# Query columns rotated once for all heads, sorts by 32, row passes on VectorE and a new order at the start of attention

## The chip, the cores and the metric

One core of a Trainium2 chip runs the whole program. The metric is the device time of one execution in microseconds. The kernel before takes 3343.34 us (median of three runs, 3342.88 to 3346.71).

## The reference

A trunk of two layers on 1024 tokens of width 1024, all in float32:

```python
for l in range(DEPTH):                                   # DEPTH = 2
    mod = silu(c) @ w_mod[l] + b_mod[l]                  # sh1, sc1, g1, sh2, sc2, g2
    h = rmsnorm(x, norm1_g[l]) * (1 + sc1) + sh1
    cq, ckv, kr, pu, cx, cb, cc, gl = split(h @ w_in[l])  # 5792 columns
    # attention: q = rmsnorm(cq) @ w_uq, 8 heads of 64 plain + 32 rotated columns;
    # k = [64 plain columns per head, 32 rotated columns shared], v 64 per head; softmax over 1024 keys
    ya = attention(cq, ckv, kr) @ w_oa[l]
    yb = pooling(pu) ; yc = short_convolution(cx, cb, cc) @ w_oc[l]
    merged = gate0 * ya + gate1 * yb + gate2 * yc        # gates = sigmoid(gl + b_gate)
    x = x + g1 * (merged @ w_out[l])
    h2 = rmsnorm(x, norm2_g[l]) * (1 + sc2) + sh2
    aff = softmax(h2 @ w_router[l])                      # 16 experts
    top_val, top_idx = top_k(aff.T, 128)                 # each expert takes its 128 best tokens
    x = x + g2 * scatter_add(swiglu(h2[top_idx]) * top_val)
return rmsnorm(x, final_g)
```

A rotation takes the two halves x1, x2 of the 32 columns to x1 cos - x2 sin and x1 sin + x2 cos.

## The kernel before, in words

Every large product is done as three matmuls (`mm3`, line 325): both factors are split (`split`, line 115) into a part `hi` that ScalarE rounds to the matmul's format and the rest `lo` that VectorE subtracts, and hi·hi + hi·lo + lo·hi are summed in PSUM. So each weight block and each activation costs one pass of ScalarE and one of VectorE.

The order of the instructions on each engine is laid out when the program is built, from the order in which they are written and from when the planner believes their inputs ready; each engine then works through its own list. `behind(ins)` puts what is written in it behind an instruction on the same engine, `gated(ins, by)` makes one wait for another. DMAs are issued from the queue of the engine named: SP for most loads, POOL for stores, ACT for some.

A layer runs through these stages:

1. Projections from `h` (held transposed, `hhi`, `hlo`), the convolution and the pooling.
2. Low-rank projections `cq`, `ckv` and the key's 32 rotated columns (lines 695 to 722), then the eight projections of the attention's gate (line 755 and after). Beside these, `w_out` is multiplied by g1 (`wk`, line 766) and gates go to DRAM (line 770).
3. Attention. A unit is one head and one tile of 128 queries: `scores`, softmax, `trans` (eight transposes, split again), and after each second unit `av`. Scores run two units ahead (LA = 2). `k_pair(hp)` makes the plain key rows of two heads and splits the pair's query weights into `qw`, in seven pieces for hi and lo. `q_head(h)` makes 128 rows of one head's query: 64 plain, 32 rotated columns, and the same 32 with their halves swapped. The rows are multiplied by a table (`tab_e` or `tab_o`: ones, cosine, signed sine) and split. The keys hold the rotated 32 rows twice (`rope_part`, one for each of four key buffers), so the product over 128 rows sums both parts of the rotation.
4. The merges: sixteen products with `w_oa` (`merge_mm`), each gated and added to the other branches (`merge_gate`). The gates come from DRAM two ahead (`gate_load`).
5. The output projection, eight tiles of 128 tokens (`out_mm`), each with a residual sum (`xo`), a norm, transposes (`x_trans`), `router`, `soft` (the 16 affinities of each token) and `h2_rows`: the normed rows go to DRAM for the experts, ScalarE scaling them, POOL multiplying by `a2` and adding `sh2`.
6. Routing. The 128 best affinities of each expert are found by sorting. `LISTS` are lists of one or two tiles, sorted by 16 rounds of "eight largest" and "replace" on 16 partitions (`top_round`). Tiles 6 and 7 take the quick way: `quick_sort` spreads the 128 tokens over four groups of 32 on 128 partitions, `quick_rounds` sorts these in four rounds, `quick_gather` brings them back to 16 partitions, `quick_list` merges them in steps of a bitonic sort, `quick_merged` merges the list into the best so far. Work of the lists is put in `fill` and taken out FILL steps at a time, twice a tile. After the last tile the threshold, the slots (`choose`, `chosen`) and the first gather follow.
7. The experts: 16 rounds of three products with 1024x1024 weights, loaded through a ring of buffers.

## Time and profile before

| | |
|---|---|
| median of three runs | 3343.34 us |
| the profiled execution | 3343.92 us |
| its span, first to last instruction | 3342.1 us |
| TensorE busy (matmul) | 3178.8 us, 15825 instructions |
| VectorE busy | 2434.5 us, 3738 instructions |
| ScalarE busy | 1857.3 us, 2535 instructions |
| POOL busy | 346.5 us, 356 instructions |
| mean granted clock of TensorE | 0.979 of full speed |

The first number is measured without the profiler; the profiled execution has its own time, and the span lies within it. Busy time is what the engine spent in instructions, without waits. In the views below, "L115" is a line of the kernel. A name such as `wlo<-raw,whi` is output and inputs. PE is TensorE's matmul, PEld its weight load, DVE is VectorE, ACT is ScalarE, SP the queue that issues most loads. "Idle before" and "waited for" name what ended an engine's idle time.

### The profile page before, as it was taken

To read this page: it belongs to the slowest core of one execution; us is meant where nothing else is said; L and a number is where in the kernel's file an instruction comes from. 1 tells how busy PE (TensorE), PEld (TensorE's weight loads), DVE (VectorE), ACT (ScalarE), POOL (GpSimd) and SP (SyncE) were. 2 spreads that over 40 slices of the span, in tenths; PEclk is the share of its full clock that TensorE was granted. 3 is DMA by queue.
4 is the path that set the end of the run, shared out by engine and by line. 5 is a ranking of instruction groups with operands and counts; after the bars stand their busy time and mean duration, and the time that the engine had idled before them with its cause. 6 is when DMAs were issued, how large, how long until landed. Compare 5 with 4: busy or idle time off the path is not lost.

```text
span 3342.1 us, 41527 instructions
## 1 busy us (share of the span) xinstructions
PE 3178.8 (95%) x15825; PEld 2616.3 (78%) x15825; DVE 2434.5 (73%) x3738; ACT 1857.3 (56%) x2535; POOL 346.5 (10%) x356
## 2 busy tenths in 40 slices
PE   6999999999997999999989999999999969999996
PEld 5888887788786788888778888887887858888875
DVE  5555525499868899999854445347998589999997
ACT  5111213488744888887631122226886448888876
POOL 2001011000023001010020000010000331001010
PEclk8999999999998999999999999999999979999998
DMA  6346334100366899999622354340005659999995
GB/s 225 120 138 205 130 125 137 64 18 7 117 221 233 314 394 380 389 389 373 245 60 82 128 165 139 104 164 24 14 28 164 227 211 366 390 390 380 387 381 182
DMA packets 279271, 685.90 MB, mean 205 GB/s; under 512 B 24934, under 2 KB 131648, under 8 KB 279072
## 3 DMA queue, kind: packets, MB, share of 16 engines
q1 hardware_dynamic: 242912, 563.13, 45.5%
q0 software_dynamic: 33856, 111.74, 10.6%
q10 hardware_dynamic: 2304, 8.39, 0.7%
q8 instruction: 124, 2.03, 0.2%
q14 instruction: 75, 0.61, 0.1%
HBM read 607.63 MB, written 75.55 MB: 204 GB/s over the span
## 4 chain that ended last, share of the span: by engine, by line
PE 79%; DVE 12%; ACT 4%; issue 2%; DMA 2%; POOL 1%; SPq 0%; POOLq 0%; DVEq 0%; ACTq 0%
PE ps L325 63%; PE pa L325 4%; PE pa L1149 4%; DVE wlo L115 4%; DVE mx L846 2%; PE pa L864 2%; PE ps L1353 1%; PE pa L872 1%; PE pa L874 1%; ACT whi L115 1%; ACT pexp L851 1%; PE pa L1189 1%; DVE af L1072 1%; DVE pexp L854 1%; DVE T L115 0%
## 5 line engine op out<-in xcount | busy, mean ns | idle before, releaser
L115 DVE TENSOR_TENSOR wlo<-rg,whi 128x1024 fp32r<-128x1024 f32 x768 | 899.6, 1220 | 97.9 <-ACT whi L115 95.1
L115 ACT CAST whi<-rg 128x1024 fp32r<-128x1024 f32 x768 | 763.8, 1048 | 180.1 <-PE ps L325 180.0
L325 PE MATMUL ps<-whi,T 128*128 128x512 f32 x3072 | 841.5, 393 | 3.6 <-ACT T L115 2.2
L325 PEld LDWEIGHTS ps<-whi,T 128*128 128x128 f32 x3072 | 574.4, 189 | 125.6 <-ACT T L115 3.1
L325 PE MATMUL ps<-wlo,T 128*128 128x512 f32 x1536 | 488.1, 399 | 5.0 <-DVE wlo L115 2.6
L325 PE MATMUL ps<-hhi,whi 128*128 128x512 f32 x1376 | 427.3, 392 | 0.0
L325 PE MATMUL ps<-hlo,whi 128*128 128x512 f32 x1376 | 424.0, 389 | 0.0
L325 PE MATMUL ps<-hhi,wlo 128*128 128x512 f32 x1376 | 423.7, 389 | 0.0
L115 ACT CAST whi<-raw 128x2048 fp32r<-128x2048 f32 (+2 forms) x63 | 108.7, 1726 | 428.0 <-PE ps L325 370.5
L325 PEld LDWEIGHTS ps<-wlo,T 128*128 128x128 f32 x1536 | 281.0, 189 | 74.3 <-DVE wlo L115 18.6
L325 PEld LDWEIGHTS ps<-hhi,whi 128*128 128x128 f32 x1376 | 256.9, 188 | 58.8 <-issue 4.2
L325 PEld LDWEIGHTS ps<-hlo,whi 128*128 128x128 f32 x1376 | 258.3, 188 | 54.2
L325 PEld LDWEIGHTS ps<-hhi,wlo 128*128 128x128 f32 x1376 | 258.3, 188 | 54.1
L115 DVE TENSOR_TENSOR wlo<-raw,whi 128x2048 fp32r<-128x2048 f32 (+2 forms) x63 | 130.1, 2065 | 99.9 <-ACT whi L115 99.8
L325 PE MATMUL ps<-khi,raw 128*128 128x512 f32 x512 | 165.8, 405 | 7.2 <-ACT pexp L851 5.7
L115 DVE TENSOR_TENSOR wlo<-pa,whi 128x512 fp32r<-128x512 f32 x256 | 169.5, 681 | 1.1 <-ACT whi L115 0.9
L851 ACT ACTIVATE pexp<-ps,nm 128x1024 f32<-128x1024 f32 x128 | 143.2, 1119 | 30.3 <-DVE nm L848 27.8
L846 DVE TENSOR_REDUCE mx<-ps 128x1 f32<-128x1024 f32 x128 | 155.0, 1213 | 4.3 <-PE ps L325 3.5
L1446 POOL DMA_INDIRECT xres<-y,idx x30 | 72.5, 2416 | 779.4 <-DVE y L1445 779.4
L115 ACT CAST whi<-pa 128x512 fp32r<-128x512 f32 x256 | 139.6, 588 | 6.2 <-PE pa L864 5.0
L229 DVE SCALAR_TENSOR_TENSOR macc<-raw,csil,macc 128x256 f32<-128x256 f32 x280 | 135.0, 484 | 8.4
L864 PE MATMUL pa<-ident,pexp 128*128 128x128 f32 x1024 | 135.2, 273 | 2.6 <-DVE nm L848 1.8
(412 smaller groups left out, 4626.9 us busy)
## 6 DMA issues: line engine op xcount, KB each, us to landing
rg<-in_w_gate_dram SPq DMA_DIRECT2D x128, 1024.0 KB, 8.9
rg<-in_w_up_dram SPq DMA_DIRECT2D x128, 1024.0 KB, 7.0
rg<-in_w_down_dram SPq DMA_DIRECT2D x128, 1024.0 KB, 7.8
raw<-in_w_mod_dram SPq DMA_DIRECT2D x48, 1024.0 KB, 5.3
raw<-in_w_in_dram SPq DMA_DIRECT2D x43, 1024.0 KB, 5.2
part<-pr POOLq DMA_DIRECT2D x32, 512.0 KB, 3.9
pr<-part POOLq DMA_DIRECT2D x16, 512.0 KB, 4.4
sq<-in_w_out_dram POOLq DMA_DIRECT2D x16, 512.0 KB, 4.7
```

The lines of the kernel that those rows point to most:

```text
L115: return ACT.copy(hi, src), DVE.tensor_sub(lo, src, f(hi))
L229: DVE.scalar_tensor_tensor(acc, raw[:, k], csil[:, k:k + 1], acc, op0=OP.mult, op1=OP.add)
L325: PE.matmul(dst[:, s], a, b[:, s], start=start and i == 0, stop=stop and i == 2)
L846: DVE.reduce_max(mx, p, axis=AX.X)
L851: ACT.activation(e, p, AF.Exp, bias=nm, scale=SCALE, accum_out=sm)
L854: DVE.tensor_scalar(e[:, :NORM_DVE], e[:, :NORM_DVE], ri, None, op0=OP.mult)
L864: PE.transpose(p[:, 128 * k:128 * k + 128], e[:, o:o + 128], ident)
L872: PE.matmul(po[:, o:o + 256], vt[:, k, h, :], phi[:, k, :], start=(k == 0), stop=False, skip_group_check=True)
L874: PE.matmul(po[0:64, o:o + 256], vt[:, k, h, 0:64], plo[:, k, :], start=False, stop=(k == 7), skip_group_check=True)
L1072: DVE.match_replace(a, v[:, 15 - r, :], a, -1.0)
L1149: PE.matmul(p[c_], a, b, start=(k == 0 and i == 0), stop=(k == 7 and i == 2))
L1446: POOL.indirect_dma_start(out=xres[l], in_=y, in_offset=None, compute_op=OP.add, out_offset=bass.IndirectOffsetOnAxis(ap=idx[e][:, 0:1], a ...
```

## The change

- Tables: `tabd` now has plain cosine, sine, and one table for the key (cosine and signed sine, twice). `krsel` writes the key's rotated rows once and zeros in the second copy.
- `q_rope`, written behind the gate projection of d = 3: from the 32 rotated columns of all heads it makes two blocks of 128 rows (first halves of all eight heads, second halves of all eight), rotates them, splits them, and stores hi and lo head by head in DRAM (`qrd`), by POOL's queue.
- `q_pair(hp)` in place of two `q_head`: the plain columns of two heads in one block of 128; the rotated rows of each head come from `qrd` by two loads of 32 partitions on SP, gated on an exponential some units back. A third query buffer `q3` is added; `q_head`'s product with a table goes, and `qw` is split in one piece.
- Start of attention: `k_pair(0)` and `q_pair(0)` are written ahead of the first value tiles; three of the four `rope_part` go into the unit loop at units 2, 9 and 17, behind an exponential; the first query weights are loaded during the gate projections.
- Merges: four products use PSUM that attention held, instead of two, and the split of `wo2` goes behind the split of the last head's output.
- Output projection: loads of the first two tiles on SP; transposes and router products written later; the rows of tiles 3 to 6 are scaled by VectorE in two instructions, those of tile 7 in a product after each half of the residual and one more instruction, ahead of the router's second half.
- Sorting: tiles 4 and 5 also take the quick way, two lists of two tiles remain, FILL goes from 4 to 6, and half of tile 6's sort is written ahead of the last softmax.
- `choose(0)` is made in two halves.

```diff
-FILL = 4
-LISTS = ((0, 2), (2, 2), (4, 1), (5, 1))
+FILL = 6
+LISTS = ((0, 2), (2, 2))
+OWN = 3
...
+            def q_rope(raw):
+                w = [W.tile([128, 3, 2, 8, 16], F32R, name=n_, tag=n_) for n_ in ("whi", "wlo")]
+                for i in range(2):
+                    split(w[0][:, :, i], w[1][:, :, i], raw[:, :, :, 16 * i:16 * i + 16])
+                w = [a.rearrange("p k i h c -> p k i (h c)") for a in w]
+                ps = []
+                for i in range(2):
+                    p = ps2()
+                    for k in range(3):
+                        mm3(p, w[0][:, k, i], w[1][:, k, i], cqhi[:, k], cqlo[:, k], k == 0, k == 2)
+                    ps.append(p)
+                cos, sin = (cp.tile([128, S], F32, name="sq", tag=n_, bufs=1) for n_ in ("sq", "rb"))
+                SP.dma_start(cos, tabd[0])
+                SP.dma_start(sin, tabd[1])
+                r = [cp.tile([128, S], F32, name="cf", tag="cf", bufs=3) for _ in range(3)]
+                hi = cp.tile([128, S], F32R, name="rhi", bufs=1)
+                for i, (a, b) in enumerate(((cos, sin), (sin, cos))):
+                    DVE.tensor_mul(r[2 * i], ps[0], a)
+                    DVE.tensor_mul(r[1], ps[1], b)
+                    (DVE.tensor_add if i else DVE.tensor_sub)(r[2 * i], r[2 * i], r[1])
+                    lo = r[2 * i].bitcast(F32R)
+                    split(hi, lo, r[2 * i])
+                    for part, src in enumerate((f(hi), r[2 * i])):
+                        POOL.dma_start(qrd[l][:, 16 * i:16 * i + 16, part, :], src)
...
+            def q_pair(hp):
+                w = [a.rearrange("p k i c -> p k (i c)") for a in qw[hp]]
+                for h in (2 * hp, 2 * hp + 1):
...
+                    r = 64 * (1 - h % 2)
+                    for o in (0, 32):
+                        ld = SP.dma_start(f(qs[h][r + o:r + o + 32]), qrd[l][h])
+                        if last_exp:
+                            gated(ld, last_exp[-4])
                 for q in range(2):
                     s_ = slice(512 * q, 512 * q + 512)
                     p = ps1()
                     for k in range(3):
-                        mm3(p, w[0][:, k, cc], w[1][:, k, cc], cqhi[:, k, s_], cqlo[:, k, s_], k == 0, k == 2)
-                    qf = ap.tile([128, 512], F32, name="pexp", tag="pexp", bufs=3)
-                    DVE.tensor_mul(qf, p, tab[:, s_])
-                    split(qs[h][:, 0, s_], qs[h][:, 1, s_], qf)
+                        mm3(p, w[0][:, k], w[1][:, k], cqhi[:, k, s_], cqlo[:, k, s_], k == 0, k == 2)
+                    for i in range(2):
+                        r = slice(64 * i, 64 * i + 64)
+                        split(qs[2 * hp + i][r, 0, s_], qs[2 * hp + i][r, 1, s_], p[r])
...
+            k_pair(0)
+            q_pair(0)
             for t in range(2):
                 v_tile(t)
-            k_pair(0)
-            q_head(0)
...
-            for i in range(1, 4):
-                rope_part(i)
             for n, (h, t) in enumerate(units):
+                if n in (2, 9, 17):
+                    with behind(last_exp[-1]):
+                        rope_part((2, 9, 17).index(n) + 1)
...
             for d in range(2):
-                merge_mm(pm[:, 512 * d:512 * d + 512], wo0, 128 * d, 0)
+                merge_mm(pms[d], wo0, 128 * d, 0)
             av(7, 3, *phl.pop((7, 3)), po[7])
+            for d in range(2, 4):
+                merge_mm(pms[d], wo1, 128 * d - 256, 0)
...
-        split(wo2[0], wo2[1], wo2_raw)
+        with behind(*last_o[-1]):
+            split(wo2[0], wo2[1], wo2_raw)
...
+                if t == 7:
+                    xn = gained.pop(t)
+                    DVE.scalar_tensor_tensor(xn, xn, rss[t], sh2, op0=OP.mult, op1=OP.add)
+                    return POOL.dma_start(h2d[l][sl, :], xn)
+                xn = op_.tile([128, D], F32, name="xn", bufs=1)
+                if t >= OWN:
+                    DVE.scalar_tensor_tensor(xn, xo, rss[t], a2, op0=OP.mult, op1=OP.mult)
+                    DVE.tensor_add(xn, xn, sh2)
+                else:
+                    with behind(softs[-1]):
+                        ACT.activation(xn, xo, AF.Copy, scale=rss[t])
+                    POOL.tensor_mul(xn, xn, a2)
+                    POOL.tensor_add(xn, xn, sh2)
...
             def aff_trans(t):
-                if t == 6:
+                if t > 3:
                     quick_sort(t)
                     quick_rounds(t)
...
             scale(t)
+            stored = h2_rows(t)
             router(t, 1)
-            quick_gather(6)
             fills(1000)
+            quick_half(6)
             ready = soft(t)
             quick_sort(t)
             quick_rounds(t)
             quick_gather(t)
+            with behind(ready):
+                quick_merged(6)
...
-            stored = h2_rows(t)
-            with behind(ready):
-                quick_merged(6)
```

## Rows read from the trace of the kernel before

**Rows 1.** The page, busy time by engine: us, share of the span, instructions.
```profile
PE 3178.8 (95%) x15825; PEld 2616.3 (78%) x15825; DVE 2434.5 (73%) x3738; ACT 1857.3 (56%) x2535; POOL 346.5 (10%) x356
```
**Rows 2.** Layer 0 by stretch: us; busy PE, PEld, DVE, ACT, POOL; PEclk, DMA, GB/s.
```profile
512.00:600.00 88.00, 88.00 (x382) 70.22 (x381) 49.37 (x34) 25.41 (x22) 12.86 (x24) 1.00 0.48 162
655.00:887.00 232.00, 229.29 (x1460) 200.04 (x1458) 216.00 (x431) 196.82 (x362) 1.60 (x3) 1.00 0.08 25
...
955.00:1062.00 107.00, 102.81 (x545) 85.10 (x545) 72.13 (x300) 51.30 (x96) 41.32 (x28) 1.00 0.56 214
1062.00:1097.00 35.00, 8.61 (x86) 7.26 (x87) 28.62 (x118) 14.13 (x27) 9.09 (x9) 0.53 0.61 217
```
**Rows 3.** TensorE's waits, whole span: waited for, us, times, longest us.
```profile
PE pa L325 <- DVE op L884: 9.8, 2, 4.9
...
PE ps L325 <- ACT pexp L851: 6.2, 8, 1.8
PE pa L1175 <- DVE xo L1154: 6.0, 4, 1.9
...
PE pa L1221 <- DVE aff L1201: 4.7, 6, 0.8
...
PE pa L1104 <- DVE aff L1201: 4.5, 4, 1.4
...
PE pa L325 <- ACT qw L115: 3.0, 2, 1.6
...
PE ps L325 <- ACT raw L115: 1.5, 2, 0.8
```
**Rows 4.** Chain of waits (start us, us, what): a query head; four gate projections, layer 1.
```profile
760.81 4.12 PE pa L325 x18
...
2203.63 43.74 PE ps L325 x192
```
**Rows 5.** VectorE by shape, 655 to 887: times, busy us, mean ns.
```profile
L115 DVE TENSOR_TENSOR raw<-pexp,raw 128x512 fp32r<-128x512 f32 x14 | 9.7, 690 | 4.8 <-ACT raw L115 4.8
...
L115 DVE TENSOR_TENSOR klo<-pa,khi 64x512 fp32r<-64x512 f32 x12 | 7.9, 682 | 0.1
L836 DVE TENSOR_TENSOR pexp<-pa,tab_o 128x512 f32<-128x512 f32 x8 | 5.5, 691 | 1.8 <-PE pa L325 1.3
```
**Rows 6.** VectorE by shape, 512 to 622.
```profile
L766 DVE TENSOR_TENSOR sq<-sq,rk 128x1024 f32<-128x1024 f32 x8 | 9.8, 1224 | 22.0 <-DMA sq<-in_w_out_dram 22.0
```
**Rows 7.** The chain of waits between attention and merges, layer 0.
```profile
901.28 1.91 ACT whi L115
...
903.21 2.29 DVE wlo L115
```
**Rows 8.** VectorE by shape, 955 to 1062.
```profile
L1070 DVE MAX8 top<-af 16x8 f32<-16x128 f32 x32 | 8.7, 276 | 0.4
...
L1201 DVE TENSOR_SCALAR aff<-aff,ri 128x16 f32<-128x16 f32 x7 | 6.6, 945 | 0.1
```
**Rows 9.** The chain of waits in the routing tail, layer 0.
```profile
1067.49 0.25 DVE aff L1201
...
1068.60 2.19 DVE ll L1090
...
1076.41 0.14 DVE ll L1089
...
1083.33 0.29 DVE ll L1295
```
**Rows 10.** POOL in order of time, 1062 to 1076.
```profile
1068.38 2.34 POOL L1211 TENSOR_TENSOR xn<-xn,a 128x1024 f32<-128x1024 f32 x1 [4.64 <-ACT xn L1210]
...
1071.14 2.33 POOL L1212 TENSOR_TENSOR xn<-xn,sh 128x1024 f32<-128x1024 f32 x1
```
**Rows 11.** DMA issues: times, KB each, median us to landing.
```profile
gh<-part SPq DMA_DIRECT2D x32, 256.0 KB, 2.9
...
tabd<-cs SPq DMA_DIRECT2D x2, 128.0 KB, 6.0
```

More of the change, by code (lines that the diff above doesn't have):

```diff
@@ L134, in encoder @@
     gate0d = [dram.tile([8, 128, S], F32, name=f"gate0{l}") for l in range(DEPTH)]
-    tabd = dram.tile([2, 128, S], F32, name="tabd")
+    tabd = dram.tile([3, 128, S], F32, name="tabd")
+    qrd = [dram.tile([8, 32, 2, S], F32, name=f"qrd{l}") for l in range(DEPTH)]
     woutd = [dram.tile([8, 128, D], F32, name=f"woutd{l}") for l in range(DEPTH)]
@@ L147, in encoder @@
     krsel = consts.tile([128, 128], F32, name="krsel")
-    for q in range(4):
+    DVE.memset(krsel, 0.0)
+    for q in (0, 2):
         for r in range(4):
@@ L292, in rope_tables @@
         DVE.tensor_scalar(sgn, sgn, 0.125, -1.0, op0=OP.mult, op1=OP.add)
-        one = ip.tile([128, S], F32, name="one", tag="ra")
-        ACT.activation(sn, sn, AF.Copy, scale=sgn)
-        DVE.memset(one, 1.0)
-        for (i, r, src) in ((0, 0, one), (0, 64, cs), (0, 96, sn), (1, 0, cs), (1, 32, sn), (1, 64, one)):
-            n = 64 if src is one else 32
-            SP.dma_start(tabd[i, r:r + n, :], src[r:r + n, :])
+        turned = ip.tile([128, S], F32, name="turned", tag="ra")
+        ACT.activation(turned, sn, AF.Copy, scale=sgn)
+        SP.dma_start(tabd[0], cs)
+        SP.dma_start(tabd[1], sn)
+        for (r, src) in ((0, cs), (32, turned), (64, cs), (96, turned)):
+            SP.dma_start(tabd[2, r:r + 32, :], src[r:r + 32, :])
     def rms_scale(src, n, scr):
@@ L770, in encoder @@
                     POOL.dma_start(gate0d[l][d], g)
+                    if d == 2:
+                        rope_raw = q_rope_load()
+                    if d == 4:
+                        uq0 = uq_load(0)
+                    if d == 3:
+                        q_rope(rope_raw)
                     if d == 1:
@@ L778, in encoder @@
         with pool("att", side="right") as ap:
+            khi, klo = ([ap.tile([128, S], F32R, name=f"{n_}{i}") for i in (2, 3)] for n_ in ("khi", "klo"))
             vt = ap.tile([128, 8, 8, 128], F32R, name="vt")
-            khi = [ap.tile([128, S], F32R, name=f"khi{i}") for i in range(4)]
-            klo = [ap.tile([128, S], F32R, name=f"klo{i}") for i in range(4)]
+            khi, klo = ([ap.tile([128, S], F32R, name=f"{n_}{i}") for i in (0, 1)] + k_ for n_, k_ in (("khi", khi), ("klo", klo)))
             raw = W.tile([128, 2, 8, 64], F32, name="raw", tag="raw")
@@ L806, in k_pair @@
             def k_pair(hp):
-                raw = ap.tile([128, 3, 192], F32, name="uq", bufs=1)
-                SP.dma_start(raw, w_uq[l][:, 192 * hp:192 * hp + 192].rearrange("(k p) f -> p k f", p=128))
-                qw[hp] = [ap.tile([128, 3, 256], F32R, name=f"qw{i}", bufs=1) for i in range(2)]
+                raw = uq0 if hp == 0 else uq_load(hp)
+                qw[hp] = [ap.tile([128, 3, 2, 64], F32R, name=f"qw{i}", bufs=1) for i in range(2)]
+                split(qw[hp][0], qw[hp][1], raw.rearrange("p k (i c) -> p k i c", c=96)[:, :, :, 0:64])
                 cc = slice(128 * hp, 128 * hp + 128)
@@ L1242, in encoder @@
                 out_mm(t, p, 0, 0, 3)
+                if t == 1:
+                    router(0, 0)
                 if t > 0:
```

98 lines of the change are left out of this document (57 added, 41 removed).

## The prediction

> **What bounds the kernel now.** I read four views in this order: busy time by stretch, what TensorE waited for, the chain of waits stage by stage, and the instructions by shape. TensorE is busy for 95% of the span [rows 1], so a microsecond counts only where TensorE works or stands. The stretches [rows 2] show three regimes. In the gate projections (512 to 600) TensorE has no gap and VectorE is busy 49.4 of 88 us. In attention (655 to 887) TensorE is busy 229.3 of 232 us, with VectorE close behind at 216.0. In the routing tail (1062 to 1097) TensorE is busy only 8.6 of 35 us at a granted clock near one half; there VectorE makes the time. The expert stage is 16 equal rounds that TensorE fills; the change touches only its first selection. Layer 1 repeats these stages, so I work per layer and double.
>
> The waits of TensorE over the whole span [rows 3] name small stalls, each figure being for two layers: 9.8 us at the start of the merges, 6.0 for the residual rows `xo`, 4.7 and 4.5 for the affinities, 3.0 and 1.5 at the start of attention.
>
> **Part by part, per layer.**
>
> *Query columns.* Before, each head has its own 128 columns (64 plain, 32 rotated, 32 swapped): 18 matmuls a head, 4.12 us [rows 4], 8 heads. After, `q_pair` makes the plain columns of two heads in one block of 18: four blocks. Attention loses 4 x 4.12 = 16.5 us of TensorE. `q_rope` makes the rotated columns of all heads in two blocks of 18, inside the gate projections, where 192 matmuls take 43.74 us [rows 4], 0.228 each: 36 x 0.228 = 8.2 us added in a stretch without a gap, so all of it counts. Its upper bound is 12.4 us, if TensorE also stands while the next gate weights are split, bounded by twice 2.1 us (1.9 on ScalarE and 2.3 on VectorE [rows 7]); I take 8.2, since the split has the 8.2 us of the new block itself as cover.
>
> *What lies beside it.* `q_rope` puts four products, an addition, a subtraction and two low parts of 128x1024 on VectorE, at 1.22 us [rows 6] 9.8 us, beside 38.6 idle us of VectorE in that stretch. If that cover were gone the two PSUM tiles that it holds would stop the next but one projection; the third PSUM slot gives it a further 10.9 us (48 matmuls). Its table loads go to SP, its four stores of 512 KB to POOL's queue among the gate stores; nobody needs the rows until attention, four projections (43.7 us) later. I cost these at nothing.
>
> *VectorE in attention.* In the stretch of 655 to 887 it loses 14 products (8 and 6 alike) and 14 low parts at 0.69 [rows 5], 19.3 us, and some 4 us of small weight pieces; it gets 12 low parts of 64x512 at 0.68, 8.2 us, and three rope parts at 1.2, 3.6 us. So about 11.5 of 216.0 go and 204.5 stay, against 212.8 of TensorE: 96% where it was 94%. The slack shrinks and I give back 1.0 us. The bounds are 0 and 4.8: if VectorE can't fill a larger share than before (216.0 of 232), the stretch ends at 204.5 / 0.931 = 219.7, and TensorE alone would allow 214.9 with its gaps.
>
> *Start of attention.* TensorE stood 1.5 us for the seven split pieces of `qw` and 0.75 for the first query (half of [rows 3]). After, the query weights are loaded in the stage before, split in one piece first, and two value tiles (12 matmuls, 2.7 us) stand between the queries and the first scores, while three of the four rope parts go behind exponentials later. What is late next is the wait on the first exponentials, up to 1.8 us [rows 3], which stays. I take -2.2, bounds 0 and -4.0 (that wait gone too).
>
> *Merges.* TensorE stands 4.9 us because the split of `wo2` (2.29 us of VectorE) stands ahead of the last head's sum `op`, whose PSUM must come free [rows 7]. After, two more merges (24 matmuls, 5.5 us) use PSUM that is already held, and the split goes behind the last head's. Then the low part of `wo2` is late: about 6 us after the last attention product, against 5.5 of cover. I take -4.4, bounds -2.4 (that split wholly uncovered) and -4.9.
>
> *Output projection.* The waits for affinities in mid stage are 4.7/2 + (4.5/2 - 1.4, which belongs to the tail) = 3.2 us [rows 3]. They come from VectorE steps that last 0.95 us on average for 128x16 [rows 8], because POOL's two passes over the rows (2.34 us each [rows 10]) run beside them. From tile 3 on those passes go to VectorE: 2 x 1.2 us for four tiles and 2.4 for the last, 12 us, in a stretch where it is busy 72.1 of 107; two lists sorted by 32 replace two of 16 rounds each (32 steps of 0.28 alone [rows 8]), about 5 us less, and steps stretched by POOL give 5 back. The move of aff_trans behind one more block covers tiles 1 to 3. Of the 3.0 us for `xo`, 1.7 are at the first tile, whose transposes move behind the rest of its block and whose load leaves ScalarE's queue for SP's, behind the last gate load; of the other 1.3, VectorE being late, I count 0.5. Against it 0.6 of additional small matmuls and 0.6 for rows that VectorE now does ahead of a softmax: 3.2 + 1.7 + 0.5 - 1.2 = -4.2. Bounds: -1.7 (only the first tile) and -5.4.
>
> *Routing tail.* From the last affinities to the last sort step VectorE takes 1067.5 to 1083.3, 15.8 us [rows 9]. Two steps of one line last 2.2 us each (one is shown, the other starts 2.75 us later) where their like takes 0.14, beside POOL's two passes for the last tile [rows 9, 10]. Those passes go: that tile's rows are multiplied with their gain right after the residual, and finished by one VectorE instruction while TensorE does the router: -4.1. Twelve sort steps of tile 6 (0.135 each) move ahead of the last softmax, into the same 2 us of waiting: -1.6; the rest fills waits, -0.3. Sum -6.0; bounds -3.6 (only the longer part of the lock goes, and the new row work delays the logits by a step) and -8.0. The Trainium skill (SBUF — State Buffer, SBUF: two separate sides) says that a GpSimd instruction holds the port pair for its whole length against a VectorE one with two SBUF inputs; the trace agrees with its 2.2 us steps. By that rule the two `rest` subtractions that stay on POOL would still cost up to 1 us, so -5.0 here.
>
> `choose(0)` in halves lets four small matmuls start early: under 0.2 us, zero. The constants and tables in the beginning lie beside DMA: zero.
>
> **Sum.** -16.5 + 1.0 + 8.2 - 2.2 - 4.4 - 4.2 - 6.0 = -24.1 a layer, -48.2 for two. The profiled execution took 3343.9 us (span 3342.1 and 1.8 around it); the median of the runs shown is 0.6 lower. 3343.3 - 48.2 = **3295 us**. All bounds on their good ends give 3282, all on their bad ends about 3330.
>
> **Rivals.**
> 1. *VectorE binds attention.* For: 94% busy already, and pair blocks come in bursts with rope parts. Against: TensorE waits only 2.7 us in 232 now [rows 2]. With the upper bound of 4.8 and the start of attention not mending (+2.2): +6 a layer, 3307. Chance 0.15.
> 2. *VectorE gets too much in the output projection.* Rows of four tiles and sorts compete; the planner may place a row pass ahead of the logits. For: one of the `xo` waits a layer is already VectorE being late [rows 3]. Against: the long lists shrink by the same amount. Output projection 0 and tail -3: +7.2 a layer, 3310. Chance 0.14.
> 3. *Slower: rope rows come late.* Each pair issues four loads of 256 KB onto 32 partitions, waiting on SP for an exponential some four units back; the first scores that need them come after four units of 3.3 us (the attention stretch of [rows 2] holds some 58 units beside seven query blocks of 4.12 and three key blocks of 2.7) and a query block, 17 us. The nearest rows with 32 partitions, 128 KB stores, landed after 6.0 us [rows 11]. If 256 KB took 12 and the four went one after another, 48 us: 31 late, three pairs, two layers, 186 us: 3295 + 186 = 3481. It decides from about 25 us for the four, where the gain is gone. Against: 256 KB loads of `gh` land in 2.9 us while others are under way [rows 11], so loads overlap. Chance 0.04. The Trainium skill (SBUF — State Buffer, Door 1: The DMA port swizzle) says that 32 neighbouring partitions reach only half of the 16 ports; from its peak of about 436 GB/s I estimate 4.8 us for the four loads, within the cover, and the sum stays. No row of before shows such a load.
> 4. *The change doesn't do what it says:* the long steps come from something else than POOL, and the tail keeps them: +4.1 and +3.2 a layer, 3310. The coincidence in time makes it unlikely: 0.04.
>
> **Chances.** Forecast 0.60, rivals 0.15, 0.14, 0.04, 0.04, several of them together (about 3322) 0.03. The range of 8 in 10 is **3280 to 3318**. A difference under 0.2% (6.7 us) can't be told from none. Slower needs rival 3 or one like it: 0.04; within 0.2%: 0.02; faster: 0.94.
>
> **What would show it.** Right: matmuls of `qw` at half the count and 36 new ones a layer in the gate projections at 0.228; attention's TensorE stretch 15 us shorter with waits under 5; no 4.9 us wait on `op`; no 2.2 us sort step, and 9 to 10 us from the last affinities to the last sort step. Wrong: TensorE waiting for the load of rope rows, or for `nm` and `pexp` by more than 5 us a layer; a gap in the gate projections.

## The result, and the profile after

The changed kernel takes 3309.7 us (median of 4 runs, 3309.2 to 3312.6) where the kernel before took 3343.6 us beside it; the ratio is 0.9899, 95% interval 0.9882 to 0.9916. That is 33.9 us, where 48.2 were forecast. The time lies inside the range.

The span of the profiled execution falls by 34.7 us, 3342.1 to 3307.4. To see where, I divide each layer at eight points of the timeline, each the start of an instruction: the first matmul of the key's rotated columns `rk`, the last gate, the last `av` matmul (of the weights' high part), the first `out_mm`, the last residual `xo`, the last affinities `aff`, the threshold behind the sort (`least`), and the last transpose of the first gathered rows. Layer 0 / layer 1, us:

| kernel | gate projections | attention | merges | output projection | to affinities | to `least` | to rows |
|---|---|---|---|---|---|---|---|
| before | 98.7 / 98.8 | 279.2 / 279.4 | 45.5 / 45.8 | 115.7 / 116.1 | 5.3 / 5.3 | 16.1 / 16.1 | 12.6 / 12.5 |
| after | 107.2 / 107.1 | 260.2 / 259.4 | 39.1 / 39.0 | 120.7 / 121.6 | 5.6 / 5.6 | 10.7 / 10.7 | 12.5 / 12.2 |
| mean change | +8.4 | -19.5 | -6.6 | **+5.3** | +0.3 | -5.4 | -0.2 |
| forecast | +8.2 | -17.7 | -4.4 | **-4.2** | 0 | -6.0 | 0 |

The stages give -17.1 and -18.4 us; +0.8 lies outside of them (+1.9 ahead of layer 0's, -2.4 between the layers, +1.3 behind). One term has the wrong sign, the output projection's; the others together came out better than forecast.

Each length is of one profiled execution, and some differ between executions in which nothing of the stage was changed. In the edits below, the time ahead of layer 0's stages is 521.8 to 526.6 us and that between the layers 1072.0 to 1075.7, so the +0.8 is within the scatter. The output projection takes 120.7 to 123.6 us in the changed kernel and the three edits that leave it alone; TensorE's mean granted clock in it is 0.96 to 0.99 there.

The page after, busy time by engine, answers to [rows 1]: TensorE loses 13 us, VectorE 18, POOL 43.

```profile
PE 3165.8 (96%) x15813; PEld 2601.2 (79%) x15813; DVE 2416.8 (73%) x3652; ACT 1845.2 (56%) x2489; POOL 303.8 (9%) x344
```

The stretches of layer 0 after, columns as in [rows 2]. Attention is compared over the same work, from the fifth to the 62nd exponential of the layer (664.0 to 875.4; before 657.0 to 884.5, second view): TensorE lacks 3.7 us in 211.4 where it lacked 2.7 in 227.5, with VectorE at 95% where it was at 93%. In the output projection (946 to 1052) it lacks 7.2 in 106, more than before (4.2 in 107).

```profile
512.00:600.00 88.00, 87.98 (x378) 69.45 (x377) 53.43 (x39) 27.58 (x25) 11.04 (x20) 1.00 0.47 141
664.00:875.40 211.40, 207.75 (x1337) 180.09 (x1336) 200.72 (x390) 189.63 (x334) 1.60 (x3) 1.00 0.14 41
946.00:1052.00 106.00, 98.77 (x539) 80.85 (x536) 70.13 (x296) 44.48 (x87) 21.45 (x19) 0.98 0.54 203
1057.00:1081.00 24.00, 5.08 (x65) 4.33 (x65) 20.41 (x92) 10.15 (x20) 3.56 (x5) 0.51 0.63 223
```

```profile
657.00:884.50 227.50, 224.79 (x1421) 195.55 (x1420) 211.50 (x422) 192.73 (x354) 1.60 (x3) 1.00 0.08 25
```

TensorE's waits in the output projection of layer 0, after (us, times, longest). Of [rows 3], the 4.9 us for `op` is gone, and of the affinities mid-stage 0.2 is left; instead the gathers of the sorted parts (`topl`) and one late residual have come.

```profile
PE pa L1174 <- DVE topl L1166: 4.0, 2, 2.8
PE pa L1238 <- DVE xo L1213: 3.4, 2, 3.0
PE pa L1252 <- DVE hT L1241: 0.8, 1, 0.8
PE pa L1292 <- DVE aff L1264: 0.2, 1, 0.2
```

Where the 3.0 us come from stands in the timeline of layer 0 (start us, us, engine, in brackets idle time and its releaser). POOL issues tile 2's store at 985.10, of the only buffer `xn`; it lands 8.6 us later, where the median of these stores is 4.0. VectorE's first pass over tile 3's rows needs that buffer and stands 3.48 us until the store has landed; the logits and the residual are queued behind it, and TensorE stands until the residual is there.

```profile
985.10 0.59 POOL L1284 DMA_DIRECT2D h2d<-xn  x1 [0.30 <-POOL xn L1283]
...
993.88 1.28 DVE L1277 SCALAR_TENSOR_TENSOR xn<-xo,rs,a 128x1024 f32<-128x1024 f32 x1 [3.48 <-DMA h2d<-xn]
...
996.76 0.22 DVE L1256 SCALAR_TENSOR_TENSOR lg<-pa,rs,shl 128x16 f32<-128x16 f32 x1
996.90 0.67 DVE L1213 TENSOR_TENSOR xo<-xo,pa 128x512 f32<-128x512 f32 x1
...
997.62 0.66 PE L1238 MATMUL pa<-ident,xo 128*128 128x128 f32 x4 [2.97 <-DVE xo L1213]
```

The chain of waits after. The 36 matmuls of `q_rope` answer to [rows 4]: 8.49 us, 8.2 forecast. Behind the last affinities, the 2.2 us steps of [rows 9] are gone; the last tile's row pass (`xn`) stands ahead of the logits, for 1.20 us.

```profile
580.10 8.49 PE ps L330 x36
...
1052.21 0.69 DVE xo L1213
...
1055.16 1.20 DVE xn L1273
...
1057.78 0.23 DVE aff L1264
...
1068.23 0.29 DVE ll L1376
1068.54 0.28 DVE least L1377
```

### The profile page after: what moved, and what is told of

Same layout as the page of the kernel before. It is cut to its first block, busy times and chain, and to the rows that moved or that the text cites. A ratio compares the mean times of both kernels' runs of the same rounds, so it can differ in the third digit from the quotient of the medians.

```text
span 3307.4 us, 41525 instructions
## 1 busy us (share of the span) xinstructions
PE 3165.8 (96%) x15813; PEld 2601.2 (79%) x15813; DVE 2416.8 (73%) x3652; ACT 1845.2 (56%) x2489; POOL 303.8 (9%) x344
## 4 chain that ended last, share of the span: by engine, by line
PE 72%; DVE 10%; issue 9%; DMA 5%; ACT 3%; POOL 1%; SPq 0%; POOLq 0%; DVEq 0%; ACTq 0%
PE ps L330 57%; PE pa L1208 5%; DVE wlo L117 3%; PE pa L330 3%; DMA raw<-in_w_mod_dram 3%; DVE macc L234 1%; PE ps L1434 1%; PE pa L915 1%; DVE mx L897 1%; ACT whi L117 1%; ACT pexp L902 1%; PE pa L923 1%; PE pa L925 1%; PE pa L1252 1%; PE ps L495 1%
## 5 line engine op out<-in xcount | busy, mean ns | idle before, releaser
L117 ACT CAST whi<-raw 128x2048 fp32r<-128x2048 f32 (+3 forms) x67 | 110.6, 1654 | 433.6 <-PE ps L330 365.7
L330 PEld LDWEIGHTS ps<-wlo,T 128*128 128x128 f32 x1536 | 280.7, 188 | 73.8 <-DVE wlo L117 18.9
L330 PEld LDWEIGHTS ps<-hhi,wlo 128*128 128x128 f32 x1376 | 258.2, 188 | 55.8 <-DVE wlo L117 1.9
L117 DVE TENSOR_TENSOR wlo<-raw,whi 128x2048 fp32r<-128x2048 f32 (+3 forms) x67 | 132.1, 1975 | 96.9 <-ACT whi L117 96.8
L915 PEld LDWEIGHTS pa<-ident,pexp 128*128 128x128 f32 x1024 | 116.9, 140 | 27.0 <-PE ps L330 9.7
```

The lines of the kernel that those rows point to most:

```text
L117: return ACT.copy(hi, src), DVE.tensor_sub(lo, src, f(hi))
L330: PE.matmul(dst[:, s], a, b[:, s], start=start and i == 0, stop=stop and i == 2)
L915: PE.transpose(p[:, 128 * k:128 * k + 128], e[:, o:o + 128], ident)
```

## The experiments

Each is an edit of the changed kernel, unless said otherwise. The intervals are those of the ratio to the kernel before; where two of them overlap, the stage lengths of the profiles show whether something moved, and where. Three dots stand for lines of an edit that are left out.

### The output projection: what makes it longer

**Tile 3's rows behind the residual.**

```diff
                     soft(t - 1)
-                    h2_rows(t - 1)
+                    if t - 1 != OWN:
+                        h2_rows(t - 1)
...
-                residual(t, p, 0)
+                added = residual(t, p, 0)
+                if t - 1 == OWN:
+                    with behind(added):
+                        h2_rows(t - 1)
```

> The changed kernel with one thing moved: VectorE's row pass of tile 3 goes behind the first half of the residual of tile 4. Theory: the rows have one buffer, the last store of a tile whose rows POOL made is late, and VectorE stands 3.5 us for it with the residual queued behind; TensorE waits 2.97 us (layer 0) and 2.46 us (layer 1) for that residual. Then both waits go, and the short fall of the granted clock after the one in layer 1: 3309.7 - 5.4 - 1 = 3303 us. Rival: VectorE has too much to do in this stage as a whole, the wait comes back at the next tile: 3309 us.

Measured: 3303.1 us, ratio 0.9872 (0.9856 to 0.9889). The output projection is 115.7 / 115.5 us, 5.0 and 6.1 shorter, and no other stage moves by more than 0.5 us. The profiled execution is the fastest of the four (3297.2), and the interval of the time still overlaps that of the changed kernel. The wait on `xo` is gone, so the row pass ahead of the residual was its cause; that the pass itself is held by the store is read from the timeline above, the store was not made faster. The waits were 3.0 and 2.5 us. Most of the rest is the clock: in the changed kernel its granted share falls to 0.50 once in this stage of layer 0 (behind the second wait on `topl`, of 2.77 us) and twice in layer 1 (behind `xo` and behind `topl`), in this kernel never, though a wait of 2.3 us on `topl` stays. The changed kernel behind `topl` in either layer and over its stage in layer 0, then this kernel's stage, where TensorE is busy 1.8 us less:

```profile
1037.00:1040.00 3.00, 3.00 (x9) 2.28 (x8) 2.97 (x8) 0.00 (x0) 0.21 (x1) 0.50 0.00 0
2665.00:2668.00 3.00, 3.00 (x10) 2.31 (x9) 2.96 (x7) 0.00 (x0) 0.04 (x1) 0.50 0.01 3
931.50:1052.20 120.70, 113.47 (x613) 93.04 (x611) 78.85 (x309) 49.85 (x97) 23.05 (x22) 0.99 0.58 213
```

```profile
927.90:1043.60 115.70, 111.71 (x609) 91.86 (x607) 79.06 (x308) 49.74 (x97) 23.04 (x22) 1.00 0.59 215
```

**The gathers half a block or more later.**

```diff
                     h2_rows(t - 1)
+                    if t > 5:
+                        quick_gather(t - 2)
+                        fill.append(lambda t=t: quick_merged(t - 2))
...
-                if t > 4:
-                    quick_gather(t - 1)
...
             router(t, 1)
+            quick_gather(6)
...
```

> The changed kernel with the gather of a tile's sorted groups written later on TensorE, in the first block of the next tile (for tile 6 behind the router of tile 7), and its merge with it. Theory: TensorE stands 1.27 and 2.77 us a layer for the sort rounds on VectorE only because the gather stands too early in its queue; both go: 3309.7 - 8.1 = 3301.6 us. Rival: VectorE is late as a whole, and what TensorE no longer waits for in mid stage it waits for in the routing tail (sort of tile 6 ends later): 3308 us, tail from the last affinities to the last sort step 13 us instead of 10.5.

Measured: 3302.3 us, 0.9864 (0.9847 to 0.9880), just below the changed kernel's interval. Output projection 117.9 / 114.7, but 8.2 / 8.1 to the affinities instead of 5.6: of the 2.8 and 6.9 gained, 2.5 come back as VectorE's work ahead of the last softmax. The layers differ by the clock, on average 0.97 in the stage of layer 0 and 1.00 in that of layer 1; the profiled execution is the slowest of the four (3309.1, the others 3300.6 to 3303.1).

**Both.**

> Both moves together: the row pass of tile 3 behind the residual, the gathers later. Theory: they are separate stalls of the output projection, so the sum: 3309.7 - 6.4 - 8.1 = 3295 us, which is what had been forecast for the change. Rival: one lateness of VectorE behind both, the second move then adds nothing: 3302 us.

Measured: 3297.2 us, 0.9851 (0.9835 to 0.9868), below the changed kernel. The output projection is 111.3 / 111.7: 4.4 below the kernel before, which is the forecast of -4.2. To the affinities it takes 9.0 / 8.9. In its waits on layer 0 the long ones on `topl` and `xo` are gone, and the last affinities wait 5.2:

```profile
PE pa L1157 <- DVE aff L1264: 5.2, 1, 5.2
PE pa L1252 <- DVE hT L1241: 1.3, 1, 1.3
PE pa L1238 <- DVE xo L1213: 0.8, 1, 0.8
```

**The sorting of tiles 4 and 5 as before.**

```diff
-FILL = 6
-LISTS = ((0, 2), (2, 2))
+FILL = 4
+LISTS = ((0, 2), (2, 2), (4, 1), (5, 1))
...
-                if t > 3:
+                if t == 6:
                     quick_sort(t)
...
-                if t > 4:
-                    quick_gather(t - 1)
...
```

> The changed kernel with the sorting of tiles 4 and 5 as it was before (whole rows of 128 by 16 partitions, four filled in at a time) and only tiles 6 and 7 sorted by 32; the last tiles' rows stay on VectorE. Theory (the gathers of the sorted parts of tiles 4 and 5 in the middle of the output matmuls cost TensorE about 4 us per layer, and these go): output projection 120.7 to 117 us, if the whole-row sorts don't make VectorE late instead. They are 16 rounds of about 0.5 us more per tile on VectorE, so the affinities wait again up to 0.8 us each as before, some 2 us per layer back: 118 to 119 us in the stage, time 3304 to 3308 us. Rival (sorting by 32 is what made VectorE's share of the output projection lighter, and the rows of tiles 3 on moved to VectorE only fit because of it): output projection 122 us or more, tail longer, time 3315 us or more.

Measured: 3308.3 us, 0.9889 (0.9873 to 0.9906), not told apart from the changed kernel. The output projection is 114.3 / 113.4, better than the theory's 118, and to the affinities it takes 11.7. The timeline of its layer 0 shows why: tile 5's last rounds stand between the last residual and the logits. Both the theory and the rival put the loss in the wrong stage.

```profile
1044.41 0.69 DVE L1213 TENSOR_TENSOR xo<-xo,pa 128x512 f32<-128x512 f32 x1 [0.17 <-PE pa L1208]
...
1053.03 0.27 DVE L1133 TENSOR_TENSOR best<-best,top 16x128 f32<-16x128 f32 x1
...
1053.63 0.22 DVE L1256 SCALAR_TENSOR_TENSOR lg<-pa,rs,shl 128x16 f32<-128x16 f32 x1
```

### The tail

**The last tile's rows on ScalarE and POOL, as before.** The diff puts tile 7 back on the path of tiles 0 to 2 and its `h2_rows` back behind the sorts.

```diff
...
-                if t == 7:
-                    xn = gained.pop(t)
-                    DVE.scalar_tensor_tensor(xn, xn, rss[t], sh2, op0=OP.mult, op1=OP.add)
-                    return POOL.dma_start(h2d[l][sl, :], xn)
...
-                if t >= OWN:
+                if OWN <= t < 7:
...
```

> The changed kernel with the rows of the last tile made as before the change: ScalarE scales, POOL multiplies and adds, after the last affinities. Theory: two sort steps of 2.2 us come back, the tail from the last affinities to the last sort step grows from 10.5 to 14.6 us, 8.2 us for two layers, less what the product after the residual cost (0.6 us twice): 3317 us. Rival: the long steps were not POOL's doing, the tail stays at 10.5: 3309 us.

Measured: 3316.4 us, 0.9907 (0.9891 to 0.9924). To the affinities 4.6 / 4.5 (1.0 less), to `least` 14.8 / 14.9 (4.1 more): the theory's numbers, in the stages; the time's interval overlaps the changed kernel's. The two long sort steps are back in its chain of waits:

```profile
1058.50 2.26 DVE ll L1143
1061.32 2.20 DVE ll L1143
```

### Attention and its start

**The order of before.**

```diff
-            k_pair(0)
-            q_pair(0)
             for t in range(2):
                 v_tile(t)
+            k_pair(0)
+            q_pair(0)
...
+            for i in range(1, 4):
+                rope_part(i)
             for n, (h, t) in enumerate(units):
-                if n in (2, 9, 17):
-                    with behind(last_exp[-1]):
-                        rope_part((2, 9, 17).index(n) + 1)
```

> The changed kernel with the first attention work in the order of before: the first two value tiles ahead of the keys and queries of the first pair, and all rope parts ahead of the units instead of among them. Theory (the reorder is worth the 2.2 us per layer of the forecast, the rest of the stage's 19.4 us is the shorter query matmuls): end of gates to last attention-times-values 262 us instead of 259.4 to 260.2, time about 3314 us. Rival (the reorder is what made the stage gain 1.7 us more than forecast, since it also takes the rope parts out of VectorE's busy start): 264 us or more in the stage and 3319 us or more. Second rival (the waits of 4.1 us at the start after the change show that the reorder only moved them): no change, 3310 us.

Measured: 3307.3 us, 0.9888 (0.9871 to 0.9904); attention 258.2 / 259.2. The second rival: the order brings nothing that can be measured. The merges take 39.0 / 38.9 us, as in the changed kernel, with no wait on `op`; that matters below.

**The rotated rows released later.**

```diff
-                            gated(ld, last_exp[-4])
+                            gated(ld, last_exp[-1])
```

> The changed kernel with the loads of the rotated query rows (those that come back head by head over 32 partitions) released by the newest softmax exponential instead of by that four units earlier. It prices the cover of these loads, which landed in 3.2 to 10.3 us with no wait of TensorE behind them. Theory (the cover of four units, some 27 us, is far more than they need, and one unit of some 6.8 us still covers the median load of 4.7 us but not the longest): attention 259 to 262 us in each layer, time 3310 to 3314 us, and a few waits of TensorE on the rope rows appear in the attention's rows. Rival (the rows are late as soon as their release moves at all, since their queue holds them behind others): waits of 5 us or more in each of 8 pairs, some 20 us per layer and 3340 us or more.

Measured: 3321.5 us, 0.9930 (0.9913 to 0.9947); attention 265.7 / 264.6, 5.4 us a layer more, which is most of the 11.8 us. Both were off: the theory had next to no loss, and the loss is about a quarter of the rival's 20 us a layer. The theory took a unit for 6.8 us; 57 of them take 211.4 us in the changed kernel, 3.7 each, so one unit is shorter than the loads' median of 4.6 us. TensorE's waits from the gates' end to the last `av` go from 2.9 to 7.8 us in small pieces, none of them named as a load; by which way the late rows make them isn't shown. The first three in this kernel:

```profile
PE pa L915 <- DVE raw L117: 2.1, 2, 1.3
PE pa L915 <- DVE nm L899: 2.0, 5, 0.9
PE pa L915 <- DVE q L117: 1.3, 1, 1.3
```

### The merges

**Their start as before:** two merges ahead of the last `av` instead of four, `wo2` split without regard to the last head.

```diff
-            pms = [p[:, 512 * i:512 * i + 512] for p in (ps2(), ps2()) for i in range(2)]
+            pm = [ps2() for _ in range(2)][1]
...
-            for d in range(2, 4):
-                merge_mm(pms[d], wo1, 128 * d - 256, 0)
...
-        with behind(*last_o[-1]):
-            split(wo2[0], wo2[1], wo2_raw)
+        split(wo2[0], wo2[1], wo2_raw)
...
```

> The changed kernel with the start of the merges as it was before: only two merges of TensorE work stand ahead of the last attention unit, and their gates come before the rest. Theory (the merges' gain is whole, nothing behind them eats it): from the last attention-times-values matmul to the first output matmul 39.1 us go back to about 45.5 in each layer, the wait on the split rows wlo of some 4 us is there again, and the time is 3309.7 + 2 x 6.5 = 3322 us. Rival (the stage is bounded by its loads of weights, so that the output projection behind it gains what the merges lose): the stage is longer, the output projection of 120 to 121 us shorter, and the time stays within 3309 to 3313 us.

Measured: 3310.5 us, 0.9895 (0.9879 to 0.9912): no difference, and not as either theory had it. The merges take 38.4 / 38.3 us, less than after the change, without any wait, though the split of `wo2` again stands ahead of `op`:

```profile
891.66 2.29 DVE L117 TENSOR_TENSOR wlo<-raw,whi 128x2048 fp32r<-128x2048 f32 x1 [1.21 <-ACT whi L117]
893.99 0.68 DVE L935 TENSOR_TENSOR op<-pa,otmp 64x512 f32<-64x512 f32 x1
```

So the edit is not needed for the 6.6 us. The program's layout of PSUM gives a second reason: before, the last head's second sum lies in bank 0, which the first merge behind it takes next; in the changed kernel, and here, it lies in bank 1. But the edit suffices without the bank. In the kernel with the order of before, above, the sum lies in bank 0 again, the new start of the merges stays, and there is no wait on `op`: the two merges that follow use PSUM that is held, and the split comes behind the sum.

```profile
888.61 0.68 DVE L935 TENSOR_TENSOR op<-pa,otmp 64x512 f32<-64x512 f32 x1
...
891.80 2.29 DVE L117 TENSOR_TENSOR wlo<-raw,whi 128x2048 fp32r<-128x2048 f32 x1 [1.12 <-ACT whi L117]
```

**The query columns alone**: the changed kernel up to the merges, with the old order of the first attention work and the old start of the merges, and the whole routing part of the kernel before. Here the sum lies in bank 0 again, and the merges start as before.

> One part of the change alone: the rotated query columns in two blocks with their rows kept head by head. The order of the first attention work, the merges' start and the whole routing (sorting, rows by ScalarE and GpSimd) are as in the kernel before. In this program the PSUM tile of the last head's last sums lies in bank 0, which the first merge matmul behind it takes next, as in the kernel before; in the changed kernel it lies in bank 1. Theory (the queries alone make the attention 19 to 20 us shorter and the gate projections 8.4 longer; the merges' 4.9 us wait is that bank, so it is back here; the routing part of the change nets nothing, since its output projection and tail sum to 137 us before and after): gate projections 107, attention 260, merges 45 to 46, output projection to least value 137 us; 2 x (8.4 - 19.4) = -22 us, 3322 us. Rival (the merges' wait goes because VectorE has less to do for the queries): merges 39 us, 3310 us. Second rival (the routing part is worth the 10 us per layer of the forecast and another loss hides it): output projection to least value 137 us but another stage shorter than after the change, 3330 us or more.

Measured: 3316.0 us, 0.9911 (0.9894 to 0.9927). Gate projections 107.2 / 107.1, attention 258.4 / 259.4, merges 46.2 / 45.0, then 136.7 / 136.5 us to `least` (before 137.1 / 137.5, after 137.0 / 137.9). The stages are as the theory has them; the time is 6 us better than its 3322. Of the 33.9 us of the change, about 29 (3344.8 - 3316.0, measured side by side) are in this part. TensorE's waits in its layer 0, from 887 to 960 (the end of the last `av` to the output projection's second tile):

```profile
PE pa L330 <- DVE op L935: 4.9, 1, 4.9
PE pa L1225 <- DVE xo L1204: 1.4, 1, 1.4
```

**The same with the new order,** which puts the sum into bank 1.

```diff
+            k_pair(0)
+            q_pair(0)
             for t in range(2):
                 v_tile(t)
-            k_pair(0)
-            q_pair(0)
```

(and the rope parts among the units)

> The same as the query columns alone, but with the order of the first attention work as changed (keys and queries of the first pair first, rope parts among the units). Undoing that order moved the time by nothing, but it puts the PSUM tile of the last head's last sums into bank 1 instead of 0. Theory (the bank decides the merges' wait): merges 38.4 to 39 us without any wait on the sum op, all else as with the queries alone, 3310 us, 12 us under it in the same call. Rival (the bank is nothing, the wait hangs on VectorE's order alone, which is the same in both): both kernels have the same merges stage, and their times differ by under 3 us.

Measured: 3321.0 us, 0.9927 (0.9911 to 0.9944). The merges are as the theory had them, 38.4 / 38.3 us, with no wait on `op`: with the old start of the merges, the bank decides it. But the time is not 12 us lower; the median is 5 higher, and no run of the one lies among those of the other, since the output projection takes 123.3 / 124.1. In the same stretch of layer 0 TensorE now has one wait:

```profile
PE pa L1226 <- DVE xo L1205: 7.0, 1, 7.0
```

The timeline shows what it hangs on. VectorE waits for the DMAs of the last gates, the rows of x are requested from ScalarE's queue only behind the last splits of the gates (938.59), and the first tile's residual waits for their landing.

```profile
935.95 0.69 DVE L1037 TENSOR_TENSOR gh<-pa,gh 128x512 f32<-128x512 f32 x1 [2.02 <-DMA gh<-gate]
...
938.59 1.35 ACTq L1284 DMA_DIRECT2D xo<-in_x_dram  x3
...
942.44 0.69 DVE L1205 TENSOR_TENSOR xo<-xo,pa 128x512 f32<-128x512 f32 x1 [2.52 <-DMA xo<-in_x_dram]
```

In the changed kernel those rows leave from SP's queue at 934.14 and the first tile's transposes stand behind its whole block, and no such wait is there. That these two edits (SP's queue, the later transposes) keep the gain of the merges is argued from this pair; they were not taken back alone.

### A faster version

**The gathers beside the next but one tile's transposes,** with tile 3's rows behind the residual:

```diff
                     x_trans(t - 1, 1)
                     scale(t - 1)
+                    if t > 5:
+                        quick_gather(t - 2)
+                        fill.append(lambda t=t: quick_merged(t - 2))
...
             x_trans(t, 1)
             scale(t)
+            quick_gather(6)
...
```

> Two edits to the changed kernel: tile 3's rows go behind the residual of tile 4 on VectorE, and the sorted parts of tiles 4 and 5 are gathered beside the second transposition of the next but one tile (half a block later than in the changed kernel, half a block earlier than with both edits of before), tile 6's right behind tile 7's second transposition. Theory (TensorE waits on topl only where the gather comes before VectorE has done the four rounds, and VectorE is late for the last affinities only by the lists that are merged in tile 7's block): output projection 111 to 113 us as with both edits of before (111.3, 111.7), last residual to last affinities 6 to 7 us instead of 9, some 2.5 us per layer better, 3292 us. Rival (VectorE's work between the last blocks is the same whatever its order, so what the projection wins the affinities lose): sum of the two stages 120 us as before, 3297 us. Second rival (half a block is too early for the rounds): waits of TensorE on topl of 1 us or more are back, 3300 us or more.

Measured: 3295.3 us, 0.9844 (0.9828 to 0.9861). Output projection 112.2 / 110.7, to the affinities 8.4: together 119.9 where the kernel with both edits had 120.5. The first rival; not told apart from that kernel.

**And the last softmax ahead of the row pass and the sorts:**

```diff
             x_trans(t, 1)
             scale(t)
-            quick_gather(6)
-            stored = h2_rows(t)
             router(t, 1)
+            ready = soft(t)
+            stored = h2_rows(t)
+            quick_gather(6)
             fills(1000)
             quick_half(6)
-            ready = soft(t)
```

> The kernel with tile 3's rows behind the residual and the gathers beside the next but one tile's transposition, and besides, tile 7's router and softmax written ahead of its row pass, of the rest of tile 5's merge and of the first sort of tile 6. VectorE's order changes in the last 8 us before the last affinities alone: the logits of tile 7 come 9 instructions earlier, the sort of tile 6 stands partly behind the affinities. Theory (those 8.4 us are VectorE's row pass of 1.26 us and some 1 to 2 us of sorting that stand ahead of the logits; behind the affinities VectorE waits for TensorE and ScalarE for some 3 us of the 10.8, and what was moved fits there): last residual to last affinities 6 us, affinities to least value 11 to 12 us, 1.5 to 2 us per layer gained, 3291 us. Rival (VectorE's list work between the last residual and the least value is what sets the end, whatever its order): the two stages still sum to 19.2 us, 3295 us.

Measured: 3293.9 us, 0.9842 (0.9829 to 0.9856). To the affinities 7.4 / 6.8, to `least` 11.7 / 11.8; the two sum to 18.9 where they summed to 19.2. What is moved behind the affinities comes back there. It beats the kernel before and the changed kernel (its interval lies below both), and isn't told apart from the last one.

## Why the prediction was right, and where it was wrong

That the total came within 15 us is in part luck: a layer lost 9.5 us against the forecast in the output projection, and 1.8 and 2.2 more than forecast came in attention and the merges. Rivals 1, 2 and 4 were priced at 3307 to 3310 us, which is what was measured, so the total alone doesn't separate them from the forecast; the stages do.

**Query columns.** Right, in both halves: 8.49 us added where 8.2 were forecast, the gate projections longer by 8.4; in attention TensorE's busy time is 14.8 us less in layer 0 after the change, and 16.9 less (270.91 to 254.06) with the queries alone, where 16.5 were forecast (15.2 and 15.8 in layer 1).

**VectorE in attention.** The give-back of 1.0 us is small as forecast: VectorE is at 95% (forecast 96%), and over the same work TensorE lacks 0.9 us more. With the queries alone it lacks 1.9 us there and with the order undone 1.8, less than before; so what is given back comes with the new order, not with the queries. Rival 1 is out. A slip of the bound: 232 - 16.5 is 215.5, not 214.9, so it was 4.2 and not 4.8.

**Start of attention.** The size of -2.2 is too small, and the reason is half wrong: I gave it to the split in one piece and to the order. From the last gate to the fifth exponential it was 35.2 us and is 31.9; with the order undone it is 32.1, with the queries alone 32.2. So nearly all of it comes with the queries, whose weights are loaded early and split in one piece in both of these kernels. With these alone TensorE's idle time from the gates' end to the last `av` falls from 8.3 to 4.3 us, the wait on `qw` among it.

**Merges.** -6.6 where -4.4 stood. The wait of 4.9 us went; the rest is the clock, which the profile before has at 0.51 from 906.2 to 910.6, right behind that wait. The reason that I gave holds, but it is one of two, each of which is enough. With the new start of the merges and the old order (bank 0) the merges take 39.0 / 38.9 us; with the old start and the new order (bank 1) 38.4 / 38.3; with both old 46.2 / 45.0 and the wait of 4.9 us. I had read from [rows 7] that PSUM must come free, and did not ask which bank: the new order moves the sum to another one by itself. The two parts of the new start, the merges put ahead and the later split, were not separated. The later low part of `wo2`, priced at 0.5 us, makes TensorE wait 0.3.

**Output projection.** This is the step that failed: "3.2 + 1.7 + 0.5 - 1.2 = -4.2" became +5.3. The waits that I counted as gone are gone: [rows 8]'s 945 ns for `aff` are 359 on average, and of the 3.2 us 0.2 is left; VectorE by shape, 946 to 1058 of the changed kernel:

```profile
L1264 DVE TENSOR_SCALAR aff<-aff,ri 128x16 f32<-128x16 f32 x8 | 2.9, 359 | 0.1
```

What I had priced at 0.6 and 0.6 us is what failed. The "rows that VectorE now does ahead of a softmax" cost 5.0 to 6.1 us a layer, not by their 2 x 1.2 us but because tile 3's first pass waits for the store of tile 2, which still comes by the slow path, and VectorE's queue stands meanwhile. Of this 3.0 and 2.5 us are TensorE's wait, and most of the rest is the lower clock in the stage, for which the sum had no term. The "additional small matmuls" cost the stage another 4 us: TensorE stands for `topl`, since the gather is put a few matmuls behind the sort. With both mended the stage comes to -4.4. That was no gift, however: 3.4 us of it return ahead of the last affinities.

**First tile.** The "1.7" for the late rows is mis-sized by its own context: it was read where the merges end late. Once they end 7 us earlier, with the loads still on ScalarE's queue, the same lateness is 7.0 us.

**Routing tail.** -5.4 of -6.0, by the mechanism forecast: with POOL's passes the steps of 2.2 us are back and cost 4.1. Rival 4 is out. The Trainium skill (SBUF — State Buffer, SBUF: two separate sides) says that a GpSimd instruction holds the shared port against such VectorE steps; both the 2.2 us steps and their absence after agree.

**Rope rows (rival 3).** Out: 256 KB over 32 partitions landed after 4.6 us in the median, 6.9 at most in the 23 of 32 loads whose landing the trace has, four issued together, and no wait of TensorE names them. Their margin is finite: three exponentials later costs 5.4 us a layer.

**Rival 2** named the place that failed and one half of its cause (a row pass ahead of the logits), with 0 us for the output projection and -3 for the tail; it was +5.3 and -5.4. Its 3310 us is the measured time by offsetting errors.

**Still open.** How much of the difference between the queries alone (0.9911) and the whole change (0.9899) is noise: the intervals overlap, though the stages of the profile say 4.9 us a layer.

## What to carry to other kernels

When a pass moves from a slow engine to a fast one whose queue others need, look first at what its operands wait for: one buffer with a store in flight stopped the whole queue for 3.5 us, and the pass itself was only 2.5. A wait that "must go" should be named with its resource, down to the PSUM bank, before an edit is credited with it; and where two edits of a change can each remove the same wait, taking back one of them shows nothing, both have to be taken back. And when a stage is shortened, ask which load of the next stage was only just in time.

## What the runs showed of the hardware

The granted clock after a wait of TensorE differs from one wait to the next. In the changed kernel's layer 1 the same wait as above (2.46 us) is followed by the lower of the two clock levels, a granted clock of 0.50 in 2624.5 to 2627.0 and 0.93 until 2630; in layer 0 a wait of 2.97 us is followed by 1.00. The waits of 2.77 us on `topl` are followed by 0.50 in both layers (1037 to 1040 and 2665 to 2668, shown with the first experiment). Windows of the changed kernel, columns as in [rows 2]:

```profile
2622.00:2624.00 2.00, 0.01 (x1) 0.00 (x0) 2.00 (x8) 0.00 (x0) 0.29 (x1) 1.00 1.02 418
2624.50:2627.00 2.50, 2.50 (x8) 2.21 (x9) 0.08 (x1) 2.47 (x6) 0.00 (x0) 0.50 1.02 403
2627.00:2630.00 3.00, 3.00 (x18) 2.46 (x17) 1.06 (x5) 0.61 (x2) 0.00 (x0) 0.93 0.16 63
```

Around the 7.0 us wait of the queries with the new order the granted clock is 0.86, in the 3 us behind it 0.50, and over the next 4 us 0.76 on average. That wait costs more than its length: the output projection is 7.6 us longer than with the queries alone (123.3 against 115.7 in layer 0), and the wait 5.6 us longer (7.0 against 1.4).

```profile
936.00:943.00 7.00, 0.22 (x1) 0.00 (x0) 4.44 (x7) 1.24 (x2) 0.00 (x0) 0.86 0.51 172
943.00:946.00 3.00, 2.81 (x9) 2.43 (x10) 0.13 (x1) 1.31 (x3) 0.00 (x0) 0.50 0.78 216
946.00:950.00 4.00, 4.00 (x20) 3.32 (x19) 0.00 (x0) 0.00 (x0) 0.00 (x0) 0.76 1.03 422
```

The second surprise is how little 32 partitions slow a load here: 256 KB of rope rows took 4.6 us in the median over the span, 256 KB of `gh` over 128 partitions 3.2:

```profile
gh<-part SPq DMA_DIRECT2D x32, 256.0 KB, 3.2
raw<-qrd SPq DMA_DIRECT2D x24, 256.0 KB, 4.6
```
